# Plane stores issued by ScalarE, joint planes, and other places for fills, tile ends and the first projection's weights in an encoder layer

## The chip, the cores and the metric

The kernel runs on one core of a Trainium2 chip. A core has a matrix engine (TensorE, here PE, with PEld for its weight loads), VectorE (DVE), ScalarE (ACT), GpSimd (POOL) and SyncE (SP). SP computes nothing: it only issues DMA transfers, in the order of its queue, and waits before an issue until what the transfer reads is made and its place is free. ACT can issue transfers too, between its own operations. The metric is the device time of one execution in microseconds (us).

## The reference

Ten tiles of 128 tokens (1024 sample and 256 prompt tokens), model width 1024, hidden width 2816 (22 blocks of 128), pass one encoder layer:

```python
def swiglu(x, w_gu, w_down):
    g, u = jnp.split(x @ w_gu, 2, axis=-1)
    return (jax.nn.silu(g) * u) @ w_down

x = x + 0.5 * rmsnorm(swiglu(rmsnorm(x, ffn1_pre), ffn1_w_gu, ffn1_w_down), ffn1_post)
h = rmsnorm(x, mix_pre)
proj = h @ w_in
...
oa = window_gqa(qa, ka, va, sink_a)
...
mix = jnp.concatenate([rmsnorm(oa, out_norm_a), rmsnorm(ob, out_norm_b)], axis=-1) @ w_out
x = x + rmsnorm(mix, mix_post)
x = x + 0.5 * rmsnorm(swiglu(rmsnorm(x, ffn2_pre), ffn2_w_gu, ffn2_w_down), ffn2_post)
return rmsnorm(x, final_norm)
```

`window_gqa` (attention A) uses rotary queries and keys; `neighbourhood_attn` (attention B) adds a learned bias table.

## The kernel before

Products run in pairs of rounded float32 numbers: `split` makes `hi` with an ACT copy and `lo` as the difference on DVE (or POOL), and every product takes three matmuls (hi·hi, hi·lo, lo·hi).

**Gate/up.** Each block f of 128 hidden columns is computed with seven products instead of eight (a Strassen scheme over the halves of the model width and of gate and up), for two chunks of tokens: chunk 0 has 256, chunk 1 has 384. A block is 14 steps, n = 7·chunk + j. `prep(f+1)` splits the next block's weights into `ah`, `al` during these steps; they come by `load(f+2)` into one of two buffers for each half, at the end of block f. Four PSUM banks serve a chunk's seven products (`BANK`): product 2 uses product 0's bank again, so ACT must first have copied `u` out (L291). Then DVE adds, ACT applies Silu, and the results `w` and `v` of the block are stored (L319) as planes in DRAM (`hd`), `w` at j = 5, `v` at j = 6. For f ≥ 11 the planes of block f - 11 are fetched back (L327, tile `back`), and POOL makes four sums (`sums`, L336 to L339), stored as `s1` to `s4`.

**Weight sums.** The down product is a seven-product scheme too, and needs sums of weight blocks: `weight_sums` loads `bx` and two `bt`, makes four sums on POOL and returns the stores of T1 to T4 into `td`. In FFN1 sums i = f // 2 are made in every odd block f, and stored behind the next store of a plane. Tiles share tags: `t` (two buffers) serves `bt`, the table's tiles `cm` and `z`, and the raw down weights `rawd`; `x` (three buffers) serves `bx`, `back`, the residual `xr` and the first `h` tiles.

**Bias tables.** `bias_tables` makes the table for attention B in DRAM during FFN1; `fill` copies pieces of `zd` and a constant `neg` into `tt`, `fill_p` copies `zp` into `ttp`. Part of these fills is handed to attention A.

**Down.** 35 pairs (product q of 7, pair of tiles p of 5) of two pieces m (six and five k-blocks), 70 numbers n. `load_w` loads and splits a weight (`rawd` to `wd`), `load_h` loads a piece of a plane (`hl`) and splits it (`hh`). When q = 4 and q = 6 end for a pair, a tile is done: `tile_done` scales by the row factor (`row_factor`, POOL, L161 and L162) and adds the residual `xr`, then `finish1` stores the row (`x1d`), normalizes it for the projection and transposes it on PE, or `finish2` writes the output.

**Mix.** The input projection (`product`, matmuls `pj`) takes weights in pieces of 128 columns: raw weights `mraw` in the pool `mixr`, split `mh` and `ml` in `mixw`. Attention A runs as a pipeline of units with projection steps and fills between them; in `rope`, four small transfers `qs<-qf` swap halves, and DVE waits for them (L691).

**What sets the order.** The code is traced in program order for each engine; a list scheduler then moves an instruction ahead where its operands allow, as far as `issue_after` (an order given by hand) and the reuse of buffers let it. All transfers are in SP's queue and are issued in its order. Thus many constant fills of `tt` stand early in SP's queue, between FFN1's loads. The bank order, `queued` and the hook for the weight sums read:

```python
    BANK = (0, 1, 0, 2, 3, 2, 3)
...
        with self.tc.issue_after(self.last_store.ins):
            while fs:
                fs.pop(0)()
...
            with tc.issue_after(gu.last_load.ins):
                gu.later += d.weight_sums(sums)
```

## Time and profile before

| what | value |
|---|---|
| median of 3 runs | 2387.31 us (2383.97 to 2388.11) |
| profiled execution, its own time | 2389.29 us |
| its span in the profile | 2387.5 us |
| mean granted clock of TensorE | 0.978 |
| FFN1 gate/up, blocks 0 to 21 | 22 to 627 us |
| FFN1 down, first to last matmul | 643.2 to 919.2 us |
| mix (projection, attention A and B, output projection) | 919 to about 1527 us |
| FFN2 gate/up | 1527 to 2097 us |
| FFN2 down, first to last matmul | 2100.1 to 2371.4 us |

Rows of the profile read as follows: a group gives line, engine, operation, output and inputs, count, then busy time and the mean of one in ns, then the engine's idle time before them and what ended it. A row of waits gives the waiting engine and line, what it waited for, the sum, the number of times and the longest. A row of the timeline gives start and length in us; a bracket gives idle time before it and its end's cause. SPq is SP's queue.

### The profile page before, as it was taken

To read this page: it belongs to the slowest core of one execution; us is meant where nothing else is said; L and a number is where in the kernel's file an instruction comes from. 1 tells how busy PE (TensorE), PEld (TensorE's weight loads), DVE (VectorE), ACT (ScalarE), POOL (GpSimd) and SP (SyncE) were. 2 spreads that over 40 slices of the span, in tenths; PEclk is the share of its full clock that TensorE was granted. 3 is DMA by queue.
4 is the path that set the end of the run, shared out by engine and by line. 5 is a ranking of instruction groups with operands and counts; after the bars stand their busy time and mean duration, and the time that the engine had idled before them with its cause. 6 is when DMAs were issued, how large, how long until landed. Compare 5 with 4: busy or idle time off the path is not lost.

```text
span 2387.5 us, 37173 instructions
## 1 busy us (share of the span) xinstructions
PE 2255.3 (94%) x13328; PEld 2063.8 (86%) x13328; DVE 1447.7 (61%) x2565; ACT 966.7 (40%) x1993; POOL 691.5 (29%) x812
## 2 busy tenths in 40 slices
PE   5899999999799998999999999799999999999997
PEld 5899999999688886788888788699999999978875
DVE  6656556656345764498655756666656666544575
ACT  5322222222244443488666754332222222243453
POOL 5111104444200102487343334622122333300011
PEclk8999999999899998999999999899999999999999
DMA  4455657677765653322433545434544655575573
GB/s 142 108 143 140 149 145 210 181 216 215 226 198 172 218 192 124 84 47 60 116 108 83 151 137 181 163 121 136 168 153 150 178 149 161 143 256 171 173 250 116
DMA packets 421322, 371.98 MB, mean 156 GB/s; under 512 B 71633, under 2 KB 340817, under 8 KB 421137
## 3 DMA queue, kind: packets, MB, share of 16 engines
q1 hardware_dynamic: 421136, 369.61, 52.1%
q8 instruction: 105, 1.72, 0.3%
q14 instruction: 81, 0.66, 0.1%
HBM read 249.85 MB, written 121.90 MB: 156 GB/s over the span
## 4 chain that ended last, share of the span: by engine, by line
PE 71%; DVE 7%; DMA 5%; issue 3%; ACT 3%; POOL 3%; SPq 1%; DVEq 0%; ACTq 0%; POOLq 0%
PE gups L279 35%; PE dps L455 16%; PE pj L615 10%; PE yps L1087 2%; PE s_ps L644 2%; PE pt L654 2%; DMA raw<-in_ffn_w_gu_dram 1%; ACT junk L153 1%; POOL rs L162 1%; DVE al L71 1%; PE o_ps L771 1%; DMA rawd<-in_ffn_w_down_dram 1%; PE ssq L1072 1%; POOL rs L161 1%; DMA td0T<-bt 1%
## 5 line engine op out<-in xcount | busy, mean ns | idle before, releaser
L279 PE MATMUL gups<-xh,ah 128*128 128x256 f32 (+1 forms) x2464 | 767.8, 312 | 25.7 <-ACT u L291 13.1
L279 PE MATMUL gups<-xh,al 128*128 128x256 f32 (+1 forms) x2464 | 763.4, 310 | 1.7 <-DVE al L71 1.7
L279 PE MATMUL gups<-xl,ah 128*128 128x256 f32 (+1 forms) x2464 | 763.2, 310 | 0.0
L279 PEld LDWEIGHTS gups<-xh,ah 128*128 128x128 f32 x2464 | 468.6, 190 | 33.0 <-ACT u L291 15.1
L455 PE MATMUL dps<-wd,hh 128*128 128x512 f32 x1540 | 479.5, 393 | 17.8 <-ACT hh L68 17.8
L279 PEld LDWEIGHTS gups<-xh,al 128*128 128x128 f32 x2464 | 468.2, 190 | 2.2 <-DVE al L71 2.1
L279 PEld LDWEIGHTS gups<-xl,ah 128*128 128x128 f32 x2464 | 469.0, 190 | 0.0
L455 PEld LDWEIGHTS dps<-wd,hh 128*128 128x128 f32 x1540 | 289.7, 189 | 79.6 <-ACT hh L68 19.3
L455 PE MATMUL dps<-wd,hl 128*128 128x512 f32 x770 | 303.4, 394 | 5.1 <-DVE hl L71 5.0
L68 ACT ACTIVATE ah<-s 128x512 fp32r<-128x512 f32 x176 | 111.2, 632 | 230.7 <-PE gups L279 128.9
L68 ACT ACTIVATE hh<-hl 128x640 fp32r<-128x640 f32 (+1 forms) x140 | 110.8, 792 | 217.7 <-DMA hl<-hd1s 65.5
L71 DVE TENSOR_TENSOR al<-s,ah 128x512 fp32r<-128x512 f32 x176 | 142.0, 807 | 81.1 <-ACT ah L68 80.0
L71 DVE TENSOR_TENSOR hl<-hl,hh 128x640 fp32r<-128x640 f32 (+1 forms) x140 | 125.0, 894 | 97.5 <-ACT hh L68 96.3
L455 PEld LDWEIGHTS dps<-wd,hl 128*128 128x128 f32 x770 | 145.1, 188 | 41.5 <-DVE hl L71 9.6
L638 POOL TENSOR_TENSOR sb<-sb,rc 128x384 f32<-128x384 f32 (+1 forms) x160 | 126.5, 811 | 154.9 <-DVE rc L636 138.4
L615 PE MATMUL pj<-xh,mh 128*128 128x512 f32 (+1 forms) x432 | 162.2, 376 | 6.4 <-ACT mh L68 6.2
L615 PE MATMUL pj<-xh,ml 128*128 128x512 f32 (+1 forms) x432 | 156.2, 362 | 0.1
L615 PE MATMUL pj<-xl,mh 128*128 128x512 f32 (+1 forms) x432 | 156.0, 361 | 0.0
L306 ACT ACTIVATE u<-u 128x256 f32<-128x256 f32 x88 | 41.4, 471 | 276.4 <-DVE u L288 273.6
L68 ACT ACTIVATE ah<-raw 128x512 fp32r<-128x512 f32 x132 | 83.3, 631 | 151.0 <-PE gups L279 101.5
L71 DVE TENSOR_TENSOR wd<-rawd,wd 128x512 fp32r<-128x512 f32 x154 | 106.2, 692 | 56.3 <-ACT wd L68 55.9
L161 POOL TENSOR_SCALAR rs<-ssq 128x1 f32<-128x1 f32 x20 | 10.0, 500 | 433.5 <-ACT junk L472 433.4
(180 smaller groups left out, 3612.5 us busy)
## 6 DMA issues: line engine op xcount, KB each, us to landing
raw<-in_ffn_w_gu_dram SPq DMA_DIRECT2D x88, 512.0 KB, 4.4
rawd<-in_ffn_w_down_dram SPq DMA_DIRECT2D x66, 256.0 KB, 3.6
bx<-in_ffn_w_down_dram SPq DMA_DIRECT2D x22, 512.0 KB, 5.2
bt<-in_ffn_w_down_dram SPq DMA_DIRECT2D x44, 256.0 KB, 3.9
rawd<-td0T SPq DMA_DIRECT2D x44, 256.0 KB, 3.3
rawd<-td1T SPq DMA_DIRECT2D x44, 256.0 KB, 3.2
tab<-tt SPq DMA_DIRECT2D x24, 384.0 KB, 3.8
hl<-hd0s SPq DMA_DIRECT2D x20, 384.0 KB, 3.2
```

The lines of the kernel that those rows point to most:

```text
L68: nc.scalar.activation(hi, src, AF.Copy)
L71: (lo_eng or nc.vector).tensor_tensor(lo, src, hi.bitcast(F32), op=ALU.subtract)
L153: c.nc.scalar.activation(junk[:, :x.shape[1]], x, AF.Square, scale=1 / 32, accum_out=ss)
L161: nc.gpsimd.tensor_scalar(r, sums[0], sums[1] if len(sums) == 2 else 0.0, EPS, op0=ALU.add, op1=ALU.add)
L279: nc.tensor.matmul(ps, w[:, k, :], x[:, k, :], start=new and k == 0 and m == 0, stop=k == 3 and m == 2, skip_group_check=not new)
L306: nc.scalar.activation(X["u"], X["u"], AF.Silu)
L455: nc.tensor.matmul(ps, a[:, k, :], b, start=i == 0 and v == 0, stop=i == HF - 1 and v == 2)
L615: state["mm"] = nc.tensor.matmul(ps[:, :n], w[:, kk, :], xs[th][:, kk, :], start=first, stop=last)
L638: nc.gpsimd.tensor_tensor(s, s, rc[:, i:i + 1].to_broadcast(list(s.shape)), op=ALU.mult)
L644: nc.tensor.matmul(o, q, kk, start=z == 0, stop=z == 1)
L654: nc.tensor.transpose(pt[:, b, :], sbs[i][:, b * 128:(b + 1) * 128], c.ident)
L1087: nc.tensor.matmul(ps, a[:, j, i * 128:i * 128 + 128], b, start=j == 0 and m == 0, stop=j == 3 and m == 2)
```

## The change

1. Stores of planes, of weight sums, of `x1d` and of the outputs are issued by ACT, `w` behind the second Silu, `v` behind the next `u`, sums and weight sums behind `g` (`queued` now follows `last_act`). A fetch is put behind the last weight load.
2. Planes are joined: (w0, v0), (s2, s1), (s3, s4) and T2 with T1, one transfer each.
3. FFN1's weight sums are made in blocks 1, 2, 4, ..., 20; in both FFNs their stores are held until the next block. The first `h` is loaded in block 21.
4. The table's remaining fills are put behind the last `qs` transfer of a rope in attention A.
5. In the down phase the gains are loaded earlier; the gain multiply of one half comes at q = 3 and 5, and of the other when a tile is done; scale and residual are one operation; squares come in halves; the last scale of `finish2` is shared between DVE and ACT.
6. The last two tiles, 4 and 6, go by DMA into the `xl` buffer and are transposed behind the first two projections' products for thirds 0 and 2. The first projection's weights are loaded at n = 60 and split at n = 64; the pools of raw and split weights alternate with one buffer each.

ACT's queue around two chunk ends in the second half of FFN1's gate/up (`ah` and `u` are the names above, `td0T` a weight sum's store, the numbers are buffers). Before:

```order
L306 ACTIVATE u<-u 128x384
L291 ACTIVATE u<-gups 128x256
L295 ACTIVATE g<-gups 128x256
L68 ACTIVATE ah<-raw 128x512
L306 ACTIVATE u<-u 128x256
L291 ACTIVATE u<-gups 128x384
L68 ACTIVATE ah<-s_5930 128x512
L68 ACTIVATE ah<-raw 128x512
L68 ACTIVATE ah<-s_5929 128x512
L295 ACTIVATE g<-gups 128x384
```

And ACT's queue now, from `v`'s store of chunk 0 in such a block to `w`'s store of chunk 1:

```order
L319 DMA hd0v_107<-v 128x2x128
L69 ACTIVATE ah<-raw 128x512
L69 ACTIVATE ah<-s_5837 128x512
L296 ACTIVATE g<-gups 128x384
L319 DMA hd0s_111<-back 128x4x128
L319 DMA hd0s_115<-sums 128x4x128
L69 ACTIVATE ah<-s_5882 128x512
L69 ACTIVATE ah<-raw 128x512
L69 ACTIVATE ah<-s_5838 128x512
L69 ACTIVATE ah<-raw 128x512
L306 ACTIVATE u<-u 128x384
L319 DMA hd0w_104<-w 128x3x128
```

The stores stand between ACT's own operations: `hd0s`, which waits for POOL's sums, ahead of four splits, and `hd0w` between Silu and the next `u`.

SP's queue at the end of FFN1's gate/up (`td0T` stores of weight sums, `rawd` and `hl` the first loads of the down phase). Before:

```order
L401 DMA td0T_193<-bt 128x512
L401 DMA td0T_171<-bx 128x512
L401 DMA td0T_182<-bx 128x512
L401 DMA td0T_204<-bt 128x512
L411 DMA rawd<-in_ffn_w_down_dram 128x512
L319 DMA hd0v_112<-v 128x3x128
L319 DMA hd0s_124<-sums 128x3x128
L411 DMA rawd<-in_ffn_w_down_dram 128x512
L319 DMA hd0s_116<-back 128x3x128
L319 DMA hd0s_120<-back 128x3x128
L411 DMA rawd<-in_ffn_w_down_dram 128x512
```

And now, from block 20's loads for the weight sums on:

```order
L400 DMA bt<-in_ffn_w_down_dram 128x512
L401 DMA bt<-in_ffn_w_down_dram 128x512
L396 DMA bx<-in_ffn_w_down_dram 128x1024
L326 DMA back<-hd0w_99 128x4x128
L326 DMA back<-hd0w_100 128x6x128
L416 DMA rawd<-in_ffn_w_down_dram 128x512
L446 DMA hl<-hd0w_97 128x768
L416 DMA rawd<-in_ffn_w_down_dram 128x512 x7
L446 DMA hl<-hd0w_99 128x640
```

No store stands between the loads any more; the first loads of the down phase follow the last fetch.

PE's queue at the end of FFN1's down phase (`dps` down products, `tr` transposes of normalized rows, `pj` projection). Before:

```order
L455 MATMUL dps<-wd,hh 128x512 x2
L455 MATMUL dps<-wd,hl 128x512
L1364 MATMUL tr<-ident,u_7143 128x128 x4
L1364 MATMUL tr<-ident,c_6914 128x128 x4
L1364 MATMUL tr<-ident,u_7199 128x128 x4
L615 MATMUL pj<-xh_8542,mh 128x512
L615 MATMUL pj<-xl_8543,mh 128x512
```

And now:

```order
L462 MATMUL dps<-wd,hh 128x512 x2
L462 MATMUL dps<-wd,hl 128x512
L1412 MATMUL tr<-ident,u_7020 128x128 x4
L636 MATMUL pj<-xh_8437,mh 128x512
L636 MATMUL pj<-xl_8438,mh 128x512
```

One group of four transposes stands between the last down product and the first projection, where there were three.

The diff, cut to what is spoken of:

```diff
-PLANES = ("w0", "v0", "w1", "v1", "s1", "s2", "s3", "s4")
+PLANES = (("w0", "v0"), ("w1",), ("v1",), ("s2", "s1"), ("s3", "s4"))
...
+    def store(self, names, f, ch, h):
-        self.last_store = self.c.nc.sync.dma_start(self.plane(name, f, ch), h.rearrange("p (r x) -> p r x", x=128))
+        self.c.nc.scalar.dma_start(self.plane(names, f, ch), h.rearrange("p (r x) -> p r x", x=128))
...
-        for b, name in zip(self.back[f, ch], ("w0", "v0")):
-            self.c.nc.sync.dma_start(b.rearrange("p (r x) -> p r x", x=128), self.plane(name, f, ch))
+        with self.tc.issue_after(self.last_load.ins):
+            self.c.nc.sync.dma_start(x.rearrange("p (r x) -> p r x", x=128), self.plane(("w0", "v0"), f, ch))
...
-        with self.tc.issue_after(self.last_store.ins):
+        with self.tc.issue_after(self.last_act.ins):
             while fs:
                 fs.pop(0)()
...
             self.product(f, ch, j)
-            if j == 5:
+            if j == 0:
+                self.queued(self.last_v)
+            if j == 4:
                 self.queued(self.later)
             if j == 6:
+                w, v = self.X["w"], self.X["v"]
+                self.queued([lambda: self.store(("w" + k,), f, ch, w)])
+                self.last_v.append(lambda: self.store(("v" + k,), f, ch, v))
...
-        return [lambda a=a: nc.sync.dma_start(self.td[a[0]][i], a[1]) for a in (("T3", b22), ("T1", b12), ("T2", b11), ("T4", b21))]
+        return [lambda a=a: nc.scalar.dma_start(self.td[a[0]][i], a[1]) for a in (("T3", b22), ("T21", x), ("T4", b21))]
...
+def split_win(c, pool, raw):
+    hi, lo = [pool.tile([128, 8, 128], F32R, name=n) for n in ("mh", "ml")]
...
+            if n == 0:
+                st["w"] = pre
+            else:
+                pool = mw if n % 2 else mr
+                st["w"] = split_win(c, pool, load_win(nc, pool, w_in, cols))
...
+    def pinned(f):
+        with tc.issue_after(state["pin"].ins):
+            f()
...
             with tc.issue_after(gu.last_load.ins):
-                gu.later += d.weight_sums(sums)
+                gu.held = d.weight_sums(sums)
+
+        def release():
+            gu.later += gu.held
+            gu.held = []
...
+        also(3, release)
         if sums is not None:
-            hooks[8] = behind
+            also(8, behind)
...
+            also(12, lambda: d.load_h(0))
...
+        gu.queued(gu.last_v)
         gu.queued(gu.later)
-        d.load_h(0)
         d.load_w(0, HF - 1)
+        d.ap = R.open("acc", 1)
         d.hp = R.open("h", 1)
-        d.ap = R.open("acc", 1)
...
+            if m and q in (3, 5):
+                y, h = d.acc[p]["c21" if q == 3 else "u"], slice(0, 512) if q == 3 else slice(512, 1024)
+                nc.vector.tensor_tensor(y, y, gpost[:, h], op=ALU.mult)
...
-        for y, h in halves:
-            nc.vector.scalar_tensor_tensor(y, y, r, gpost[:, h], op0=ALU.mult, op1=ALU.mult)
+        nc.vector.tensor_tensor(y, A[b if second else a], gpost[:, h], op=ALU.mult)
+        r = row_factor(c, [A[a, "ss"], A[b, "ss"]])
         yield 1
-        for y, h in halves:
-            nc.vector.tensor_tensor(x[:, h], x[:, h], y, op=ALU.add)
-        yield from finish(t, x, gnext, halves)
+        for z, h in zip((A[a], y) if second else (y, A[b]), halves):
+            nc.vector.scalar_tensor_tensor(x[:, h], z, r, x[:, h], op0=ALU.mult, op1=ALU.add)
+            ss.append(square(c, x[:, h], junk_bank()))
...
-        gu.run(f, block_hooks(gu, f, {6: behind} if 1 < f < HF else {}, f // 2 if f % 2 else None))
+        gu.run(f, block_hooks(gu, f, {6: behind} if 1 < f < HF else {}, f // 2 if f == 1 or f % 2 == 0 else None))
...
+    def first_split():
+        state["pre"] = split_win(c, state["mr"], state["raw"])
...
-        elif t == PAIRS[-1][0]:
+            if t in (PAIRS[-2][0], PAIRS[-1][0]):
...
+        for _, h in halves:
+            nc.vector.tensor_tensor(x[:, h], x[:, h], gain[:, h], op=ALU.mult)
+        r = row_factor(c, ss)
...
+        nc.vector.tensor_scalar(x[:, a], x[:, a], r, None, op0=ALU.mult)
+        nc.scalar.activation(x[:, b], x[:, b], AF.Copy, scale=r)
```

More of the change, by code (lines that the diff above doesn't have):

```diff
@@ L178, in __init__ @@
         self.xb = [[None] * 7 for _ in CHUNKS]
-        self.A, self.raw, self.back, self.later = {}, {}, {}, []
+        self.A, self.raw, self.back, self.later, self.held, self.last_v = {}, {}, {}, [], [], []
         self.work = None
@@ L581, in load_win, with parts @@
     return raw
+def split_win(c, pool, raw):
+    hi, lo = [pool.tile([128, 8, 128], F32R, name=n) for n in ("mh", "ml")]
+    def parts():
+        for k in range(0, 8, 2):
+            split(c, hi[:, k:k + 2], lo[:, k:k + 2], raw[:, k:k + 2], c.nc.gpsimd)
+            yield
+    return hi, lo, parts()
 def mix_attention(c, tc, xt, w_in, sink, cosT, sinT, maskA, tt, ttp, oAd, oBd, mw, L, R,
-                  close_left, open_out, late, mr, raws, fills):
+                  close_left, open_out, late, mr, pre, fills):
     nc = c.nc
@@ L591, in mix_attention @@
     ready = set()
+    count = {"n": 0}
     def product(cols, evac):
@@ L598, in fetch @@
         def fetch():
-            st["raw"] = raws.pop(cols[0][0]) if cols[0][0] in raws else load_win(nc, mr, w_in, cols)
-            st["w"] = [mw.tile([128, 8, 128], F32R, name=n) for n in ("mh", "ml")]
+            n = count["n"]
+            count["n"] += 1
+            if n == 0:
[3 more added lines that the diff above has]
+                st["w"] = split_win(c, pool, load_win(nc, pool, w_in, cols))
         def part(i):
-            hi, lo = st["w"]
-            s = slice(2 * i, 2 * i + 2)
-            split(c, hi[:, s], lo[:, s], st["raw"][:, s], nc.gpsimd)
+            next(st["w"][2], None)
         def mm(th, k0):
             n = TH[th][1]
-            hi, lo = st["w"]
+            hi, lo, _ = st["w"]
             if k0 == 0:
@@ L1229, in down_phase @@
             q, p, m = d.seq[n]
-            if n == 30:
-                gpost = load_gain(c, G, post, "ga", scale=0.5)
-                gnext = load_gain(c, G, nxt, "gb")
-            if n == 60:
-                last()
+            if n == 20:
+                with tc.issue_after(d.last_h.ins):
+                    gpost = load_gain(c, G, post, "ga", scale=0.5)
+                    gnext = load_gain(c, G, nxt, "gb")
+            if n in last:
+                last[n]()
             if m == 0 and q in (4, 6):
@@ L1376, in finish1 @@
         yield 1
-        xn = [y for y, _ in halves]
-        if "xt" not in state:
-            state["xn"][t] = xn
-        elif t == PAIRS[-1][0]:
-            th, off = third(t)
-            x = state["xt"][1][th][:, :, off:off + 128].bitcast(F32)
-            for k, y in enumerate(xn):
-                nc.sync.dma_start(x[:, 4 * k:4 * k + 4], y.rearrange("p (k x) -> p k x", x=128))
-            state["xn"][t] = [x[:, 4 * k:4 * k + 4] for k in range(2)]
-            state["late"] = transposes(t)
-        else:
-            state["xn"][t] = xn
-            yield from transposes(t)
-    down_phase(gu, lambda t: rows(xs, xp, t), i["ffn1_post"], i["mix_pre"], finish1, open_xt)
+        xn = state["xn"][t] = [y for y, _ in halves]
+        if "xt" in state:
+            if t in (PAIRS[-2][0], PAIRS[-1][0]):
+                th, off = third(t)
+                x = state["xt"][1][th][:, :, off:off + 128].bitcast(F32)
+                for k, y in enumerate(xn):
+                    nc.sync.dma_start(x[:, 4 * k:4 * k + 4], y.rearrange("p (k x) -> p k x", x=128))
+                state["xn"][t] = [x[:, 4 * k:4 * k + 4] for k in range(2)]
+                state["late"].append(transposes(t))
+            else:
+                yield from transposes(t)
+    down_phase(gu, lambda t: rows(xs, xp, t), i["ffn1_post"], i["mix_pre"], finish1, {60: open_xt, 64: first_split})
     R.close(4)
-    mw = L.open("mixw", 2)
+    mw = L.open("mixw", 1)
     mo = MixOut(c, L, R, i["w_out"][0], (i["out_norm_a"], i["out_norm_b"]), oAd, oBd, x1d, x2d, xnd, i["mix_post"], i["ffn2_pre"])
@@ L1398, in encoder @@
     mix_attention(c, tc, state["xt"], i["w_in"][0], i["sink_a"], i["cosT"], i["sinT"], i["maskA"], tt, ttp, oAd, oBd,
-                  mw, L, R, lambda: L.close(4), mo.open, lambda: list(state["late"]), state["mr"], state["raws"], later)
+                  mw, L, R, lambda: L.close(4), mo.open, lambda: [list(x) for x in state["late"]], state["mr"], state["pre"], later)
     c.ps.use(y=(2, 3, 4, 5), tr=(6, 7, 0, 1))
```

96 lines of the change are left out of this document (51 added, 45 removed).

## The prediction

> **What bounds the kernel now.** I read the page's first and fourth parts, then tables of stretches, then the waits, then single stretches of the timeline.
>
> ```profile
> PE 2255.3 (94%) x13328; PEld 2063.8 (86%) x13328; DVE 1447.7 (61%) x2565; ACT 966.7 (40%) x1993; POOL 691.5 (29%) x812
> PE 71%; DVE 7%; DMA 5%; issue 3%; ACT 3%; POOL 3%; SPq 1%; DVEq 0%; ACTq 0%; POOLq 0%
> ```
>
> PE holds 71% of the chain, and the change leaves its matmuls as they are. What can be won is PE's idle time, 2387.5 - 2255.3 = 132 us, and the lower clock behind long gaps. A table of stretches (start and end, length, then busy time of PE, PEld, DVE, ACT, POOL, granted clock, DMA share, GB/s) finds the places:
>
> ```profile
> 82.70:626.90 544.20, 522.31 (x3529) 516.60 (x3527) 316.23 (x520) 139.18 (x271) 154.55 (x137) 0.99 0.64 173
> 627.00:643.30 16.30, 0.23 (x2) 0.09 (x1) 3.63 (x6) 3.40 (x6) 4.70 (x5) 0.65 0.93 280
> 643.30:650.00 6.70, 6.70 (x18) 5.03 (x19) 4.58 (x6) 3.67 (x6) 0.00 (x0) 0.59 0.94 303
> 920.00:940.00 20.00, 9.34 (x26) 6.62 (x27) 10.36 (x15) 7.41 (x18) 8.63 (x14) 0.57 0.34 115
> 1000.00:1140.00 140.00, 136.13 (x856) 119.00 (x857) 125.01 (x363) 116.21 (x327) 102.77 (x178) 0.98 0.26 57
> 1578.80:2096.90 518.10, 516.71 (x3517) 515.73 (x3515) 314.86 (x523) 146.45 (x276) 141.21 (x129) 1.00 0.52 158
> 2371.40:2387.50 16.10, 0.00 (x0) 0.00 (x0) 6.53 (x10) 3.02 (x6) 2.44 (x6) 0.64 0.18 65
> ```
>
> The first and sixth rows are blocks 1 to 21 of gate/up in FFN1 and in FFN2, the same matmuls: 544.2 against 518.1, so FFN1 loses **26.1 us**. The second and third are the passage into FFN1's down phase: 16.1 idle, then 6.7 us at clock 0.59, of which 41% or 2.8 are lost. The fourth is the passage out of it: 10.7 idle, some 3 more to the clock. The fifth is attention A, where DVE is busy 125 of 140 us. The last is the tail, 16.1 without a matmul.
>
> Why FFN1 loses is in the groups of that stretch (count, busy time, mean ns, idle time before and what ended it):
>
> ```profile
> L279 PE MATMUL gups<-xh,ah 128*128 128x256 f32 (+1 forms) x1176 | 365.4, 311 | 20.2 <-ACT u L291 12.7 <-DVE v L288 7.3
> L68 ACT ACTIVATE ah<-raw 128x512 fp32r<-128x512 f32 x60 | 37.7, 628 | 73.9 <-DMA raw<-in_ffn_w_gu_dram 45.5 <-PE gups L279 28.4
> ```
>
> PE waits for `u`, which ACT copies out of the bank that the third product needs; ACT waits for the next block's weights, whose splits stand ahead of that copy. One such stall in the timeline, SP's queue, then ACT, and two rows of SP's waits:
>
> ```profile
> 157.69 0.38 SPq L228 DMA_DIRECT2D raw<-in_ffn_w_gu_dram  x1
> 158.11 5.36 SPq L550 DMA_DIRECT2D tt<-in_neg_dram  x1
> 163.56 0.56 SPq L319 DMA_DIRECT2D hd0w<-w  x1
> ...
> 169.65 0.66 SPq L228 DMA_DIRECT2D raw<-in_ffn_w_gu_dram  x1
> 167.34 0.63 ACT L68 ACTIVATE ah<-raw 128x512 fp32r<-128x512 f32 x1 [5.92 <-DMA raw<-in_ffn_w_gu_dram]
> 168.29 0.36 ACT L291 ACTIVATE u<-gups 128x256 f32<-128x256 f32 x1
> SPq L319 <- DVE w L302: 261.7, 63, 11.7
> SPq L228 <- DVE s L257: 154.9, 28, 20.1
> ```
>
> The first weight load was issued at 157.69 and its split began 9.65 later, with a fill and stores beside it; the second load came behind them, 12 us after the first. In all SP stood 261.7 us at stores whose `w` was not made yet, with loads queued behind.
>
> **The change, term by term,** against the profiled run (span 2387.5, its own time 2389.3, which is 2.0 above the median shown and 1.2 above the highest).
>
> *Gate/up of FFN1.* Stores leave SP, so a weight load waits for its own buffer alone. A block of the second half had 12 stores and 4 fetches of planes and now has 8 and 2, of the same bytes, and 11 table fills, 17 constant ones and 16 small ones leave for attention A. Of the 26.1, block 1 keeps about 4: its loads go out behind block 0, at 82.7, which the change leaves. New in even blocks 12 to 20: ACT stands at the `hd0s` stores until POOL's four sums are made, with four splits and `u` behind, and POOL now has four weight sums ahead of them. Estimated from the block's start: `bx` waits about 8 us for its buffer and lands in 5 to 6 (row below), eight POOL operations take 8 x 1.13 (154.55 / 137) = 9, four splits 4 x 0.63 = 2.5: 25 to 26. PE needs `u` at 24.5 + 2 x 1.4 = 27.3 (a block, then two products of 256 of 640 columns, 24.5 x 0.4 / 7 each), less 0.4 for the copy. The margin is 1 with a scatter of 2, so I charge 0.8 five times, 4. Gain 26 - 4 - 4 = **-18** (-7 to -26). What the store alone delays at a chunk's end:
>
> ```profile
> bx<-in_ffn_w_down_dram SPq DMA_DIRECT2D x22, 512.0 KB, 5.2
> L319 SPq DMA_DIRECT2D hd0w<-w x44: 359/384/2207, 59.6 to 626.3; - x44
> 602.76 0.52 ACT L306 ACTIVATE u<-u 128x384 f32<-128x384 f32 x1 [2.51 <-DVE u L288]
> 603.58 0.38 ACT L291 ACTIVATE u<-gups 128x256 f32<-128x256 f32 x1 [0.30 <-PE gups L279]
> ```
>
> An issue of 0.38 us goes between these two, where ACT is idle for 0.30; PE asks for `u` 1.4 us after it could start, 1.0 after the copy's end, so some 0.9 of slack stays and the median costs nothing. The longest, 2.2, costs 2.2 - 0.3 - 1.0 = 0.9. No row shows a joint store's issue: by two single ones it is 0.8, still inside, and it stands at a place with more room (behind `g`). FFN2 gets these stores as well, and its row has 1.4 us idle in 518: **+1** (0 to 5, a few long issues).
>
> *Into FFN1's down phase.* Before, the loads of the first `rawd` wait for the buffers of td's last stores:
>
> ```profile
> 630.54 0.39 SPq L401 DMA_DIRECT2D td0T<-bt  x1
> 635.26 0.63 ACT L68 ACTIVATE wd<-rawd 128x512 fp32r<-128x512 f32 x1 [6.97 <-DMA rawd<-in_ffn_w_down_dram]
> 642.32 0.84 ACT L68 ACTIVATE hh<-hl 128x768 fp32r<-128x768 f32 x1 [0.98 <-DMA rawd<-in_ffn_w_down_dram]
> ```
>
> Now the last weight sums are block 20's, stored early in block 21, and ten loads and the first `hl` come during block 21, as in FFN2. So PE starts at once. Late next is `hh` of the second piece: on ACT it stands behind the last `hd0s` stores, which wait for four POOL sums behind the last `v`. From the last `gups`: 1.5 for `v`, 4 x 1.1 for the sums, 0.9 for two issues, 0.8 for `hh`, so 8; PE's first piece has 18 matmuls at 0.227 (30.2 / 133, a row below), 4.1. Idle 4, clock and the next weights 4: 19 becomes 8, **-11** (-4 to -17). FFN2's passage, in the same order:
>
> ```profile
> 2096.90:2110.00 13.10, 11.20 (x50) 9.01 (x51) 8.50 (x12) 5.00 (x8) 3.38 (x3) 1.00 0.77 228
> 2100.10:2133.50 33.40, 31.16 (x135) 24.53 (x134) 15.87 (x21) 14.50 (x23) 3.38 (x3) 1.00 0.89 281
> 721.20:751.40 30.20, 30.20 (x133) 24.79 (x132) 14.52 (x20) 10.59 (x17) 0.00 (x0) 1.00 0.53 167
> ```
>
> There four pairs end 36.6 us after the last `gups`, where four undisturbed ones (last row) take 30.2: 6.4 lost, which is also a check on the 8. It too loses stores in front of its loads, and gets the same `hh` behind stores: **-2.5** (+2 to -5).
>
> The Trainium skill, "TensorE: Matmul & The Clock Gate", section "What's actually happening", has the clock fall to half after an idle window of about 3.4 us. The trace agrees as far as it goes: 0.59 behind the gap of 16.1, 1.00 in FFN2's passage with short ones. By that rule an idle time of 4 in one piece may cost clock, and in shorter pieces the sum would be some 2 us lower.
>
> *Down pairs.* Where DVE fills up, pairs stretch; four that took 30.2 above take here:
>
> ```profile
> 819.10:852.00 32.90, 31.59 (x138) 25.09 (x137) 29.93 (x46) 18.64 (x34) 8.48 (x14) 1.00 0.84 281
> ```
>
> DVE is busy 29.9 of 32.9. A tile's work on it stays about as long (four operations, gain multiplies and sums in another pairing), but one gain multiply moves ahead to q = 3 and 5. **-3** for both FFNs (+3, if the order only shifts the crowd, to -6).
>
> *Out of the down phase.* Two waits of PE:
>
> ```profile
> PE tr L1364 <- DVE c L1375: 4.5, 1, 4.5
> PE pj L615 <- ACT mh L68: 6.2, 1, 6.2
> ```
>
> Both go: the transposes of the last two tiles stand behind projection products, and the first projection's weights are split within the down phase. Late next are the second projection's weights: their buffer lies where the last `h` tiles are, so the load goes out behind the last matmul. PE has 24 matmuls of the first projection, 24 x 0.227 = 5.4, and four transposes; the load of 512 KB takes 4 to 5 (as `bx`), its first split under 1. So 0 to 3 of 13.7 stay: **-12** (-4 to -14).
>
> *Attention A* gets the 44 fills, on the queue that carries its ropes' transfers:
>
> ```profile
> L688 SPq DMA_DIRECT2D qs<-qf x60: 507/582/1349, 973.1 to 1100.8; - x60
> tt<-in_neg_dram SPq DMA_DIRECT2D x7, 192.0 KB, 9.3
> ```
>
> 60 transfers are 15 ropes in 128 us, one every 8.5. A fill goes out behind one rope's transfers and took up to 9.3 to land in FFN1 (share 0.64); at 0.26 it should be gone before the next rope. DVE has 15 of 140 us to hide what is left. **+3** (0 to +12, 1 us at twelve ropes).
>
> *Tail.*
>
> ```profile
> 2374.20 1.41 DVE L1469 SCALAR_TENSOR_TENSOR xr<-xr,rs,gb 128x512 f32<-128x512 f32 x2 [2.31 <-POOL rs L162]
> 2375.53 0.68 DVE L466 TENSOR_TENSOR c<-c,dps 128x512 f32<-128x512 f32 x1
> ```
>
> The last sum `c` starts 4.1 us after the last matmul (2371.4), behind the tile before it, whose last DVE step waits for `rs`; now less of that tile is left. Gain and addition merge (about 1.4 less), the last multiply is shared with ACT (0.7 less): **-6** (-3 to -7.5).
>
> Sum: -18 + 1 - 11 - 2.5 - 3 - 12 + 3 - 6 = -48.5; 2389.3 - 48.5 = 2340.8, and about 1 less on the median's scale: **2340**.
>
> **Rivals.** (a) *The loads stay late*, because the 16 engines and not SP's order set their landing. For it: 9.65 us above, and share 0.64 in FFN1; against it: the fills leave FFN1, and FFN2 at 0.52 has no stall. Gate/up then gains 5 and the passage 6: 2340 + 13 + 5 = 2358. The Trainium skill, "DMA: Bandwidth & Descriptors", section "Issuing engines are not separate DMA queues", is on this side: a second issuer saves only the time to initiate a transfer. The rows of SP's waits show another cost, order in one queue. (b) *Fills hit the ropes* at twelve of 15: +12 in place of +3, 2349. (c) *The new place does not do what it is for*: ACT's waits at `hd0s` hold `hh` until the passage is as long as before (+11), and hold `u` 3 us in each of five blocks (+11): 2362. (d) *Slower*: issues on ACT take longer than the 0.3 + 1.0 us of room at each of 88 chunk ends. All 49 us are gone at 0.55 more than that, an issue of 1.85 every time; at 2.2 it costs 88 x 0.9 = 79, and the time is 2419. For it speaks the maximum of 2.2 and the 5.36 of a fill; against it the median of 0.38.
>
> **Numbers.** Forecast (2322 to 2349) 0.63; (a) 0.15; (b) 0.09; (c) 0.08; (d) 0.04; 0.01 for anything else. A measurement of this kernel tells about 0.2% (5 us) from no change. Of (a), (c) and the rest 0.04 may run on to within 0.2%, which leaves faster 0.92, same 0.04, slower 0.04. The range 2322 to 2366 takes in (a), (b) and (c); the low end has 18 us more, with gate/up, the passage and the pairs near their best.
>
> **What would show it.** Right: FFN1's 21 blocks in under 530 us and ACT's wait for `raw` below 20; the first `dps` within 2 us of the last `gups`, then one gap on `hh` below 6; `pj` straight behind `tr`; a tail near 10. Wrong: `u` released by a store or by POOL; `qs` waits of DVE in attention A above 10 us; FFN2's 21 blocks above 525; `raw` landing in 8 us without fills beside it.

## The result and the profile after

The changed kernel takes **2403.39 us** (median of 4 runs, 2403.16 to 2406.25), the kernel before 2386.39 on the same chip (4 runs, 2383.97 to 2388.11). The ratio is 1.0075, 95% interval 1.0057 to 1.0092: slower by 0.75%, where 2340 and faster had been predicted. The profiled execution has a span of 2401.4 us, 13.9 above that of before.

First the table of stretches after (start and end, length, busy time of PE, PEld, DVE, ACT, POOL, clock, DMA share, GB/s): blocks 1 to 21 of gate/up in FFN1, the first down pair, attention A, blocks 1 to 21 in FFN2, its first down pair, the tail.

```profile
77.20:609.50 532.30, 518.91 (x3530) 515.05 (x3529) 322.33 (x522) 143.25 (x274) 162.55 (x138) 1.00 0.62 168
609.80:622.80 13.00, 10.72 (x35) 7.93 (x35) 6.75 (x10) 4.98 (x9) 3.58 (x3) 0.79 0.81 259
959.10:1163.60 204.50, 168.20 (x893) 139.24 (x894) 130.41 (x371) 122.73 (x335) 98.36 (x179) 0.86 0.34 77
1594.10:2112.20 518.10, 518.10 (x3529) 517.77 (x3529) 320.22 (x528) 147.60 (x277) 148.02 (x129) 1.00 0.53 158
2112.40:2128.20 15.80, 10.18 (x34) 7.73 (x33) 5.57 (x9) 4.48 (x7) 3.02 (x3) 0.78 0.59 193
2388.40:2401.40 13.00, 0.08 (x1) 0.00 (x0) 5.90 (x10) 3.80 (x10) 3.56 (x6) 0.70 0.22 81
```

Two stretches of before in the same table, attention A from its first `s_ps` to its last `o_ps`, and FFN2's blocks 1 to 21:

```profile
1000.10:1146.50 146.40, 142.63 (x894) 124.60 (x895) 128.48 (x371) 119.38 (x335) 103.66 (x179) 0.98 0.25 56
1578.80:2099.90 521.10, 518.68 (x3528) 517.71 (x3527) 317.86 (x528) 148.65 (x279) 141.21 (x129) 1.00 0.52 158
```

Attention A runs the same matmuls 58.1 us longer. PE idles 204.5 - 168.2 = 36.3 instead of 3.8 us, and its busy time is 25.6 longer, at a clock of 0.86 instead of 0.98. All else together got 44 us shorter. By stage, cut at PE's first and last matmuls (us; the parts of the mix that are left out differ by 0.3 together):

| stage | before | after | difference | predicted |
|---|---|---|---|---|
| start to end of FFN1 gate/up | 626.8 | 609.5 | -17.3 | -18 |
| passage and first down pair, FFN1 | 16.4 + 10.3 | 0.3 + 13.0 | -13.4 | -11 |
| other 34 pairs, FFN1 | 265.3 | 268.8 | +3.5 | -1.5 |
| out of the down phase | 13.9 | 0.6 | -13.3 | -12 |
| **attention A** | 146.4 | 204.5 | **+58.1** | +3 |
| FFN2 gate/up, all blocks | 572.5 | 567.5 | -5.0 | +1 |
| passage and first down pair, FFN2 | 0.2 + 9.0 | 0.2 + 15.9 | +6.9 | -2.5 |
| other 34 pairs, FFN2 | 262.0 | 259.8 | -2.2 | -1.5 |
| tail | 16.5 | 13.3 | -3.2 | -6 |

The groups of FFN1's blocks after, as shown of before:

```profile
L280 PE MATMUL gups<-xh,ah 128*128 128x256 f32 (+1 forms) x1176 | 363.9, 309 | 13.4 <-DVE v L289 11.9 <-ACT u L292 1.0 <-ACT ah L69 0.5
L69 ACT ACTIVATE ah<-raw 128x512 fp32r<-128x512 f32 x60 | 37.8, 631 | 61.8 <-PE gups L280 58.4 <-DMA raw<-in_ffn_w_gu_dram 2.3 <-issue 1.1
```

ACT's wait for `raw` fell from 45.5 to 2.3, and PE's for `u` from 12.7 to 1.0: the stall of the prediction is gone. In attention A, PE's two largest waits, then the transfers in that stretch (KB each, median us to landing):

```profile
PE o_ps L792 <- DVE st L687: 14.2, 8, 3.6
PE s_ps L665 <- DVE stk L72: 12.9, 7, 3.3
...
tt<-zd SPq DMA_DIRECT2D x11, 384.0 KB, 7.9
...
tt<-in_neg_dram SPq DMA_DIRECT2D x6, 192.0 KB, 17.5
```

PE waits for DVE, with DVE itself busy 130 of 204 us. DVE's own two largest waits in that stretch are for engines, and none that the profile shows there is for a rope's `qs`:

```profile
DVE pl L72 <- ACT ph L69: 32.7, 26, 6.8
DVE qf L714 <- POOL qf L711: 15.6, 7, 4.4
```

DVE's queue at one rope, after and then before:

```profile
1018.65 1.30 DVE L712 TENSOR_TENSOR qs<-qs,sin 128x512 f32<-128x512 f32 x1
1019.88 0.41 DVE L687 TENSOR_TENSOR st<-o_ps,of 64x256 f32<-64x256 f32 x1
1022.67 0.69 DVE L714 TENSOR_TENSOR qf<-qf,qs 128x512 f32<-128x512 f32 x1 [2.39 <-POOL qf L711]
1024.06 1.41 DVE L72 TENSOR_TENSOR stk<-qf,stk 64x512 fp32r<-64x512 f32 x2 [0.69 <-ACT stk L69]
```

```profile
1030.11 0.79 DVE L691 TENSOR_TENSOR qs<-qs,sin 128x512 f32<-128x512 f32 x1
1031.00 0.56 DVE L71 TENSOR_TENSOR pl<-pt,ph 128x384 fp32r<-128x384 f32 x1
...
1032.68 0.67 DVE L693 TENSOR_TENSOR qf<-qf,qs 128x512 f32<-128x512 f32 x1
1033.27 0.74 DVE L71 TENSOR_TENSOR pl<-pt,ph 128x256 fp32r<-128x256 f32 x2
...
1035.57 2.19 DVE L71 TENSOR_TENSOR stk<-qf,stk 64x512 fp32r<-64x512 f32 x2 [0.68 <-ACT stk L68]
```

Before, a rope's links stood apart, with the softmax of other units between them. After, only one `st` stands between them, and DVE waits for POOL and ACT inside the chain. So two things changed in attention A: slow fills are in it, and every engine's order is another. The change orders only the fills by hand; the rest of the loop is left to the scheduler. The experiments had to tell the two apart.

### The profile page after: what moved, and what is told of

The parts are those of the page before. It is cut to its first block, busy times and chain, and to the rows that moved or that the text cites. A ratio compares the mean times of both kernels' runs of the same rounds, so it can differ in the third digit from the quotient of the medians.

```text
span 2401.4 us, 36895 instructions
## 1 busy us (share of the span) xinstructions
PE 2273.8 (95%) x13328; PEld 2072.3 (86%) x13328; DVE 1458.6 (61%) x2575; ACT 982.4 (41%) x2043; POOL 709.0 (30%) x812
## 3 DMA queue, kind: packets, MB, share of 16 engines
q10 hardware_dynamic: 130688, 91.25, 12.4%
## 5 line engine op out<-in xcount | busy, mean ns | idle before, releaser
L280 PE MATMUL gups<-xh,ah 128*128 128x256 f32 (+1 forms) x2464 | 764.9, 311 | 18.6 <-DVE v L289 13.5
L280 PEld LDWEIGHTS gups<-xh,ah 128*128 128x128 f32 x2464 | 466.7, 189 | 24.5 <-DVE v L289 15.8
L69 ACT ACTIVATE hh<-hl 128x768 fp32r<-128x768 f32 (+1 forms) x140 | 110.6, 791 | 209.6 <-DMA hl<-hd0s 55.3
L72 DVE TENSOR_TENSOR hl<-hl,hh 128x768 fp32r<-128x768 f32 (+1 forms) x140 | 124.6, 891 | 106.3 <-ACT hh L69 106.3
L462 PEld LDWEIGHTS dps<-wd,hl 128*128 128x128 f32 x770 | 145.8, 189 | 44.2 <-DVE hl L72 12.6
```

What stands on the lines that cost most here:

```text
L69: nc.scalar.activation(hi, src, AF.Copy)
L72: (lo_eng or nc.vector).tensor_tensor(lo, src, hi.bitcast(F32), op=ALU.subtract)
L280: nc.tensor.matmul(ps, w[:, k, :], x[:, k, :], start=new and k == 0 and m == 0, stop=k == 3 and m == 2, skip_group_check=not new)
L462: nc.tensor.matmul(ps, a[:, k, :], b, start=i == 0 and v == 0, stop=i == HF - 1 and v == 2)
```

## The experiments

The stages of all runs (us; cut as above; time is the median or that of one run; the last column is the kernel before on the same chip, and the experiments come from four chips). Pinned fills are those that the change puts behind a rope's last `qs`. The new orders are those that the engines have in attention A with pinned fills, the old ones those without:

| run | FFN1 gate/up | down 1 | att. A | down 2 | time | before |
|---|---|---|---|---|---|---|
| changed kernel | 609.5 | 281.8 | 204.5 | 275.7 | 2403.4 | 2386.4 |
| e1 fills not pinned | 635.4 | 284.2 | 146.1 | 274.5 | 2372.8 | 2384.2 |
| e6 e1, PE's new order | 633.0 | 285.1 | 180.1 | 274.6 | 2402.8 | 2384.2 |
| e2 pinned, PE's old order | 607.5 | 283.8 | 205.6 | 274.4 | 2403.5 | 2384.2 |
| e3 changed, `h` pool first | 607.7 | 283.4 | 204.1 | 265.4 | 2392.3 | 2384.2 |
| e7 constants in FFN1 | 631.8 | 287.0 | 202.5 | 267.6 | 2421.1 | 2385.7 |
| e8 fills in down 1 | 610.2 | 349.6 | 146.5 | 266.2 | 2403.3 | 2385.7 |
| e9 e8, stores on SP | 620.4 | 342.3 | 145.4 | 265.6 | 2405.4 | 2385.7 |
| e10 fills issued by ACT | 609.2 | 284.9 | 207.6 | 267.7 | 2400.1 | 2393.5 |
| e12 only constants pinned | 618.1 | 283.6 | 184.0 | 267.8 | 2387.6 | 2393.5 |
| e13 e1 with `h` first | 645.3 | 282.2 | 145.3 | 265.6 | 2370.0 | 2393.5 |
| e14 third `st` buffer | 610.7 | 284.6 | 199.1 | 266.6 | 2391.1 | 2384.1 |
| e15 constants read from `zd` | 608.6 | 283.3 | 192.1 | 267.0 | 2381.3 | 2384.1 |
| e17 pinned, four old orders | 609.3 | 282.8 | 205.2 | 266.7 | 2398.2 | 2385.2 |
| e18 no fills, four new orders | 637.4 | 285.8 | 202.9 | 267.0 | 2423.8 | 2385.2 |
| **e19 e17, constant rows** | 611.0 | 284.0 | 158.2 | 266.5 | **2350.2** | 2385.2 |
| e20 e13, constant rows | 623.7 | 283.3 | 146.3 | 265.6 | 2350.7 | 2385.2 |
| e21 e8, constant rows | 612.4 | 304.4 | 145.8 | 267.0 | 2360.6 | 2388.4 |
| e16 e13, old tile end | 647.6 | 279.7 | 146.4 | 269.8 | 2379.6 | 2388.4 |

### Are the pins the cause? e1, e6, e2

```diff
 e1
-                    todo.insert(4 * n + 3, (0.0, lambda f=fills.pop(0): pinned(f)))
+                    todo.insert(4 * n + 3, (0.0, fills.pop(0)))
 e6: e1, and e2: the changed kernel, both with an order for PE
+    with given_order(tc, mybir.EngineType.PE, ORDER):
         for j in range(4):
```

> The changed kernel, its table fills not put behind the ropes: the scheduler places them in FFN1 again, and PE's order in attention A is the one of before. Theory O (the fills behind the ropes made the scheduler give PE another order, projection products in runs of up to 27, and PE idles later) and theory T (the fills' transfers and their issues hold up the small transfers of attention A) both say: attention A, from the first s_ps to the last o_ps, goes from 204.5 back to 146 to 150 us. FFN1's gate/up, which ends at 609.5, then shows what the fills cost there: 0 to 15 us more. Time 2345 to 2360. If neither holds (the weight pools of one buffer each, or the stores on ACT, slow attention A), it stays near 200 and the time near 2400.

> The kernel of e1_no_pin (no fills in attention A), with PE's order in attention A given by hand as the changed kernel has it, instruction for instruction. Theory O: attention A takes 190 to 205 us with no fill near it. Theory T: 146 to 152.

> The changed kernel, fills behind the ropes, with PE's order in attention A given by hand as the kernel before has it. Theory O: attention A takes 146 to 155 us although all fills run beside it. Theory T: 190 to 205. If both have a part, the two runs split the 58 us.

e1 puts the fills (43 in the trace: 11 copies from `zd`, 16 constant ones, 16 copies from `zp`) back where the scheduler had them, in FFN1. Attention A is whole again, FFN1's gate/up ends 26 us later, above the 0 to 15 expected, and the kernel beats the one before: 2372.8 us, not the 2345 to 2360 expected, ratio 0.9951 (0.9936 to 0.9965). So the pins cost the 58, and FFN1's gain hangs on the fills' leaving: with them back its gate/up is 8.6 longer than in the kernel before. e6 and e2 did not separate order and fills: PE's new order alone costs 34, and with PE's old order the fills still cost 59. They hold one engine's order; the other three stayed with the scheduler.

### FFN2's first pair: e3

```profile
2096.29 0.33 SPq L446 DMA_DIRECT2D hl<-hd1w  x1
2101.55 9.18 SPq L416 DMA_DIRECT2D rawd<-in_ffn_w_down_dram  x5
2118.21 0.82 SPq L446 DMA_DIRECT2D hl<-hd1w  x2
```

```profile
SPq L446 <- POOL sums L337: 2.9, 1, 2.9
SPq L446 <- DMA hd1w<-w: 2.6, 1, 2.6
```

These are SP's queue and its waits in the changed kernel around FFN2's passage: the second `hl` goes out 6 us behind the last `gups`, because its place is that of gate/up's work tiles, whose sums POOL has yet to make and whose stores have yet to land. The change had swapped the opening of the pools `h` and `acc`, which moved `h` onto them. The edit swaps it back in FFN2:

```diff
+        if last:
+            d.ap = R.open("acc", 1)
         d.hp = R.open("h", 1)
+        if not last:
+            d.ap = R.open("acc", 1)
```

> The changed kernel, with the pool of h opened before that of the sums again in FFN2's down phase (in FFN1 as changed). Theory P (the swapped pools put h over the gate/up tiles, so the first loads of h wait for the last stores and sums): the first pair of FFN2's down phase, 15.9 us, goes to 8 to 10 and the gap of 5.6 goes; the time is 6 to 8 us below the changed kernel's. Theory A (hh stands on ACT behind the last stores): the first pair stays at 14 to 16.

FFN2's first pair fell from 15.86 to 7.49 us, and down 2 from 275.7 to 265.4; the time of this one run fell by 11, more than the 6 to 8 expected. The place of `h` was the cause. All runs below have this edit. In FFN1 the pools stay as in the change, and the first pair stays at 12.4 to 14.6 us, but for e9 (9.2, below).

### What a fill costs, and where: e7, e12, e8, e10, e14

```diff
 e7: the constant parts not pinned, zd and zp pinned; e12 the reverse, with PE's old order
+    for f in fills:
+        f(z=False)
+    fills = [lambda f=f: f(neg_=False) for f in fills]
 e8: nothing in attention A; in FFN1's down phase
+    {60: open_xt, 64: first_split, **{8 + 3 * n: f for n, f in enumerate(later)}}
 e10: e2 with the fills issued by ACT
-        nc.sync.dma_start(tf[:, :, a, rh, e0 * 32:e0 * 32 + 256], ...)
+        e.dma_start(tf[:, :, a, rh, e0 * 32:e0 * 32 + 256], ...)
 e14: e2 with
+        st = k.tile([64, 256], F32, name="st", bufs=3)
```

> The changed kernel with h's pool first in FFN2's down phase (as e3_h_first), and of the fills behind the ropes only the copies from zd and zp left there; the constant ones (tt<-neg) are placed by the scheduler, early in FFN1. Theory N (the constant fills, which take 13 to 17 us to land, clog the transfers wherever they are): attention A falls from 204.5 to 150 to 170 us, and FFN1's gate/up, which ended at 609.5, ends 10 to 25 us later. Theory Z (any fill on SP's queue holds up attention A's stores and rope transfers): attention A stays at 180 to 205 and gate/up ends near 612.

> The reverse of e7_neg_early, with PE's order of before: the constant fills (tt<-neg) behind the ropes, the copies from zd and zp placed by the scheduler, in FFN1. From e7 (gate/up to 631.8 with the constant ones early) the constant fills cost FFN1 about 22 us and the copies about 4; so gate/up should end at 610 to 616. Attention A: e7 had 202.5 with the copies alone; if the constant fills are harmless there it takes 146 to 155, if any fill costs there, 165 to 190.

> The changed kernel with h's pool first in FFN2's down phase and the 15 groups of fills issued by SP in FFN1's down phase, one at every third of 70 steps from step 8, each behind the load of the newest h. Theory P (fills cost where short transfers are waited for within a few us; the down phase has its next pieces loaded ahead): gate/up ends at 607 to 612, the down phase takes 282 to 295 us, attention A 146 to 150, FFN2's first pair 7.5; time 2335 to 2350. Theory T (44 fills cost 26 to 58 us wherever they run): the down phase takes 310 to 340 us; time 2360 to 2390.

> The kernel of e2_pinned_old_order (fills behind the ropes in attention A, PE's order of before) with h's pool first in FFN2, and the fills of attention A issued by ACT, behind the rope's first copy, in place of SP. Theory S (on SP's queue the fills stand ahead of the stores oAd<-st and the rope's qs, whose landings they hold up; e2 took 205.6 us there): with another queue attention A falls to 150 to 170 us, and oAd lands in at most 6 us. Theory E (the 16 DMA engines are filled, whichever queue issues; or ACT, busy 119 of 146 us, is held up by the issues): it stays at 185 to 215.

> The kernel with pinned fills and PE's old order in attention A (attention A 205.6 us there), h pool opened first in FFN2, and a third buffer for the tile st that oAd's stores read. Theory 'buffer': the fills stall attention A through late oAd stores that keep st's two buffers (DVE st <- DMA oAd 9.2, PE o_ps <- DVE st 35.5); with three buffers most of that goes, attention A 165 to 185, total about 2375. Theory 'everywhere': what is late is every short transfer of the ropes and outputs, and the wait only moves to qs and the clock; attention A stays 195 to 206, total about 2393. FFN2's first pair near 7.5 us in both.

e7: the constant parts alone cost FFN1 24 us (631.8 against 607.7), and attention A, with the copies alone, still takes 202.5. That is not the copies' doing. They and what runs beside them land fast in e7, and DVE's largest wait is that of the changed kernel:

```profile
tt<-zd SPq DMA_DIRECT2D x11, 384.0 KB, 4.1
oAd<-st SPq DMA_DIRECT2D x39, 64.0 KB, 2.1
DVE pl L72 <- ACT ph L69: 32.7, 26, 7.7
```

The engines' orders in e7 are the new ones, but for a few swaps, so what e7 measures is those. e12 has the constants alone, with 184.0; e10 and e14 have all fills. These three have PE's old order and the scheduler's for the other engines, so they too price fill and order together.

e8: 349.6 against about 283 without fills, and attention A whole (146.5). So the down phase was no cheap place. The Trainium skill, "DMA: Bandwidth & Descriptors", section "Issuing engines are not separate DMA queues", has transfers of every issuer run on the same 16 engines, so that a second issuer saves only the time to start one. e10 agrees: with the fills issued by ACT attention A takes 207.6 against 205.6 us, and the constant ones of 192 KB still land in 14.6. So it is not SP's queue that makes them slow. (e9, below, shows a gain of another kind from a second issuer: loads that no longer stand behind stores.) e14: a third buffer for `st` brings 6.5 us of the 59, so the stall is not that one buffer.

### Order or transfers: e15, e17, e18, e19

e15 reads the constants from rows of `zd`, so each row from an address of its own, and its table lacks the constant. e17 and e18 hold PE, DVE, ACT and POOL, in the projection and attention A, to the order of the other case. e19 is e17 with 384 constant rows in DRAM:

```diff
 e15
-                nc.sync.dma_start(tf[:, :, a, rh, lo * 32:hi * 32], src)
+                nc.sync.dma_start(tf[:, :, a, rh, lo * 32:hi * 32], zf[:, :, 384:384 + n])
 e17 (pinned fills), e18 (fills not pinned)
+    with given_order(tc, ORDER):
         with in_order(tc, mybir.EngineType.DVE):
 e19
-                src = bass.AP(tensor=neg.tensor, offset=neg.offset, ap=[[0, 16], [0, 24], [1, n]])
+                src = neg.rearrange("(q x) n -> q x n", x=24)[:, :, :n]
```

> As the run with pinned fills and PE's old order (attention A 205.6 us), h pool first in FFN2, but the constant fills of tt (early and pinned ones) read rows of zd, each from an address of its own, in place of the one constant row read 384 times; rows, sizes and places written are the same, the table's constant entries are wrong. Theory 'one source': many reads of the same few hundred bytes are what is slow; landing of these fills falls from 10 to 17 us to below 5, oAd's longest from 16 to below 8, attention A to 160 to 180 (the zd copies still cost some), gate/up of FFN1 5 to 10 earlier. Theory 'small rows': 384 rows of 128 to 512 bytes written to scattered places are slow whatever is read; landing stays 9 to 17 and attention A 195 to 210.

> Pinned fills in attention A as in the change, h pool first in FFN2, and the orders of PE, DVE, ACT and POOL in the projection and attention A held to those of the kernel without pins. Theory 'order': the scheduler, which counts the pinned fills as time, put the engines' work in a bad order, and the transfers themselves cost little; attention A 146 to 160, total 2335 to 2350, the fastest so far. Theory 'transfers': the fills' own traffic delays oAd and qs whatever the order; attention A 190 to 206, total 2385 to 2395. Between them (165 to 185) both count.

> The reverse: no fill in attention A (they are in FFN1, whose gate/up then takes about 640), h pool first in FFN2, and PE, DVE, ACT and POOL in the projection and attention A held to the orders that the pinned fills gave. Theory 'order': attention A 190 to 205, total about 2420. Theory 'transfers': 146 to 155, total about 2372. TensorE's new order alone had given 180.

> As e17, with the constant as 384 rows in DRAM, so that each row of a constant fill of tt reads an address of its own; the table is right. Theory 'one source': oAd's and qs's longest landings fall below 6 us; attention A falls to 146 to 150 if e17 is above it, and is within 3 of e17 if e17 is near 150. FFN1's gate/up, which keeps 17 constant fills, 0 to 6 us earlier than in e17 (609).

Transfers in attention A in e17, then in e19 (KB each, median us to landing):

```profile
tt<-zd SPq DMA_DIRECT2D x11, 384.0 KB, 7.7
oAd<-st SPq DMA_DIRECT2D x38, 64.0 KB, 2.4
qs<-qf SPq DMA_DIRECT2D x24, 64.0 KB, 4.9
tt<-in_neg_dram SPq DMA_DIRECT2D x6, 192.0 KB, 16.2
```

```profile
tt<-zd SPq DMA_DIRECT2D x11, 384.0 KB, 3.9
oAd<-st SPq DMA_DIRECT2D x38, 64.0 KB, 2.1
qs<-qf SPq DMA_DIRECT2D x24, 64.0 KB, 2.0
tt<-in_neg_dram SPq DMA_DIRECT2D x6, 192.0 KB, 4.3
```

The same bytes to the same places land in 4.3 instead of 16.2 us when each row has a source of its own, and the `zd` copies beside them in half the time. Fills from one row cost attention A 59.9 us under the old orders (e17 against e13). DVE's waits in attention A, first e17, then e18, then e19's row for the same transfers:

```profile
DVE qs L786 <- DMA qs<-qf: 24.8, 4, 11.4
DVE st L761 <- DMA oAd<-st: 22.3, 6, 5.1
```

```profile
DVE pl L72 <- ACT ph L69: 32.5, 25, 7.7
DVE qf L806 <- POOL qf L803: 14.6, 7, 4.4
```

```profile
DVE qs L786 <- DMA qs<-qf: 2.3, 3, 1.0
```

Attention A by fills and orders:

| | old orders | new orders |
|---|---|---|
| no fills | 145.3 (e13) | 202.9 (e18) |
| fills from one row | 205.2 (e17) | 204.1 (e3) |
| only copies from `zd` and `zp` | not run | 202.5 (e7) |
| fills from 384 rows | 158.2 (e19) | not run |

Each cause is enough alone, by its own waits: in e17 DVE waits for transfers, in e18 for engines, with no fill near. They don't add, and so a run that takes away one alone finds little. In the changed kernel the waits are those of e18: its orders hide the slow fills. With both gone the fills cost 13 us, above the 146 to 150 us expected for attention A. Most of that is one wait of ACT in e19, which PE then waits for, for weights of the projection that SP issues behind the last fills:

```profile
ACT mh L69 <- DMA mraw<-in_w_in_dram: 12.1, 1, 12.1
```

In e15 the fills land in about 4 us too, but attention A takes 192.1 in place of the 160 to 180 expected, with PE's old order and the other engines' left to the scheduler. The stretch in e19, against the changed kernel's row above:

```profile
963.10:1121.20 158.10, 141.78 (x893) 123.16 (x894) 128.31 (x371) 119.22 (x335) 103.54 (x179) 0.97 0.42 99
```

The DMA share is higher than in the changed kernel, 0.42 against 0.34. The share did not show this cost; the landings did.

e19 takes 2350.21 us (2349.03 to 2355.70), ratio 0.9860 (0.9845 to 0.9874), and is, with e20 (2350.73 in one run on the same chip), the fastest version measured.

### The same source in FFN1 and in the down phase: e20, e21

```diff
 e13, e8
-                src = bass.AP(tensor=neg.tensor, offset=neg.offset, ap=[[0, 16], [0, 24], [1, n]])
 e20, e21
+                src = neg.rearrange("(q x) n -> q x n", x=24)[:, :, :n]
```

> e1_no_pin and e3_h_first together: fills placed by the scheduler, h's pool first in FFN2's down phase. Each alone gave 2372.8 and 2392.3 (the changed kernel 2403.4), so if their gains of 30.6 and 11 add, 2362; if they share something, 2364 to 2372.

> The fills in FFN1 (unpinned, gate/up 635 to 645 us there, 609 without them), h pool first in FFN2, and the constant as 384 rows. Theory 'one source': the constant fills are what costs FFN1 its 26 to 35 us; gate/up ends at 610 to 620, total 2345 to 2355. Theory 'order of one queue, or bytes': gate/up stays 630 to 645, total about 2370.

> The fills in FFN1's down phase (349.6 us there with the one constant row, 282 to 287 without fills), h pool first in FFN2, the constant as 384 rows. Theory 'one source': down phase 284 to 300, attention A 146, gate/up 610; total 2336 to 2353, perhaps the fastest. Theory 'transfers in a busy place': h, w and fills share the engines and the down phase stays above 320; total above 2370.

ACT's wait in FFN1's blocks in e13, then in e20; last, PE's in the down phase in e8 and e21:

```profile
L69 ACT ACTIVATE ah<-raw 128x512 fp32r<-128x512 f32 x61 | 38.4, 630 | 75.4 <-PE gups L280 49.2 <-DMA raw<-in_ffn_w_gu_dram 18.0 <-DMA bx<-in_ffn_w_down_dram 3.0
```

```profile
L69 ACT ACTIVATE ah<-raw 128x512 fp32r<-128x512 f32 x61 | 38.4, 630 | 53.3 <-PE gups L280 48.5 <-issue 3.9 <-DVE al L72 0.6
```

```profile
PE dps L462 <- ACT hh L69: 53.5, 11, 11.3
```

```profile
PE dps L462 <- ACT hh L69: 12.3, 6, 3.2
```

FFN1's gate/up with unpinned fills varies between runs: e1, e6, e13, e16 and e18 have one order on every engine and in SP's queue there, and take 633.0 to 647.6. e20, in that same order and with only the source changed, takes 623.7, so the rows bring 9 to 24 us (14 against e18, on the same chip), and ACT's wait for `raw` falls from 18.0 to below the 0.6 of the last row shown. Some 14 remain, more than expected (610 to 620). In the down phase the cost falls from 66 to 21 (304.4 against 283), above the 300 expected. e13 was expected at 2362; it takes 2370.0, on a chip where the kernel before takes 2393.5, ratio 0.9905 (0.9889 to 0.9922). e21 has 0.9872 (0.9849 to 0.9895).

### ACT's stores alone, and the tile end: e9, e16

```diff
 e9: stores of planes and weight sums
-        self.c.nc.scalar.dma_start(self.plane(names, f, ch), ...)
+        self.last_store = self.c.nc.sync.dma_start(self.plane(names, f, ch), ...)
 e16: tile_done, finish1 and finish2 as before the change
-            if m and q in (3, 5):
-                nc.vector.tensor_tensor(y, y, gpost[:, h], op=ALU.mult)
```

> The kernel of e8_fills_down_sp with all stores of planes and weight sums issued by SP again, as before the change; planes joint, weight sums in even blocks and held. Theory F (FFN1's gate/up gained because the fills left it): gate/up ends at 605 to 615. Theory Q (it gained because the loads no longer stand behind stores in SP's queue): it ends at 618 to 630. FFN2's gate/up tells the same: 572.5 us before, 567.5 with the change.

> The kernel without pins and with the h pool first in FFN2 (down phases 282.2 and 265.6 us, tail 13.5), but with the tile end of before: both gain multiplies, the sums and the squares when a tile is done, outputs' last scale on DVE and stored by SP. Theory 'new tile end helps the tail alone': down phases within 1.5 of those, tail 15.5 to 16.5. Theory 'new tile end stretches the pairs' (an early gain multiply and two squares in ACT's and DVE's queues): down phases 3 to 5 shorter, tail 15.5 to 16.5. Theory of the prediction (pairs gain 1.5 for each FFN): down phases 1 to 3 longer.

With stores on SP, FFN1's gate/up is 10.2 us longer (620.4 against 610.2), with ACT waiting 23.7 us for `raw`; FFN2's is 568.6 against 568.0. But FFN1's down phase is 7.3 shorter (342.3 against 349.6, with the fills in both), 3.9 of it in the first pair, 9.2 in place of 13.1: `hh` no longer stands behind stores in ACT's queue, and PE's wait for it there falls from 2.6 to 0.5. So ACT's issue is worth 10 in FFN1's gate/up, gives some 4 of it back at the start of the down phase, and is worth nothing in FFN2.

The old tile end makes FFN2's down phase 2 to 4 us longer (269.8; the 14 runs with the new one and `h` first take 265.4 to 267.8) and the tail 3.4 (16.9 against 13.5). FFN1's down phase is 2.5 shorter than in e13, 1.0 of it in the first pair; other runs with the new tile end and no fills there take 281.8 to 287.0, so this is hardly more than their spread. None of the three theories holds in both phases.

## Why the prediction was wrong

**The step that failed** is the term "*Attention A* gets the 44 fills", +3 (0 to +12). Measured: 58.1. It asked what the fills do to ropes whose order stays. The order of attention A had changed on all four engines, and that alone costs 57.6 (e18 against e13); the changed kernel shows the waits of e18 and none for `qs`. The part ahead of the prediction says that a scheduler sets the order, but compares orders only in FFN1 and at the down phase's end; the prediction took that of attention A as given. Why the scheduler chose this one, I only argue: it seems to charge the fills to the queue that the ropes need, and so puts ropes late.

The price of the fills was wrong as well, and would have cost as much under the old orders (59.9, e17). The term took 9.3 us for the most that a fill needs to land in FFN1; the row's figure is a median, and the longest there took 20.7. It let this shrink at a DMA share of 0.26; in attention A it was 17.5. e19, e20 and e21 show that the slow landing belongs to the one source row, in each of three places. And it counted the ropes' `qs` alone, not the `oAd` stores, for which DVE waited 22.3 us in e17. Its count was off by one: the trace has 16 constant fills and not 17, so 43.

Rival (b), fills hit the ropes at +12, named one of the two mechanisms, at a fifth of its size; the changed kernel does not show it, since its orders hide it. Rival (d), slower by ACT's issues, gave the right sign by a wrong mechanism: nothing in the trace or e9 bears it out.

**FFN1 gate/up** (-18, measured -17.3): right in size, in part by luck. The term gave most of the gain to the stores' leaving SP's queue. Stores on ACT are worth 10 once the fills are gone (e9), but with the fills still in FFN1 the changed gate/up takes 633.0 to 647.6 (e6 to e16), 6 to 21 more than the 626.8 of before's one trace, and why was not tried. The fills' leaving makes 24 to 38. That block 1's start at 82.7 is one "which the change leaves" was wrong: it is 77.2, and 77.1 to 78.8 in every run whose constant fills leave FFN1, 81.7 to 82.6 where they stay; that is 5.5 of the 17.3. Blocks 1 to 21 took 532.3, above the 530 named as a sign of being right. The sum for `u` behind the `hd0s` stores is 24.5 to 25.5, not 25 to 26; PE waited 1.0 us for `u` in all, not the 4 charged. Rival (a), landings set by the 16 engines, was half right: the fills slowed what ran beside them, but SP's order counts too (e9).

**FFN2's comparison row** ended 3 us early, and so does the stage in the table of before: the last `gups` is at 2099.9, not 2096.9. So FFN2's blocks took 521.1, FFN1 lost 23 rather than 26.1, and the passage 3.4 rather than 6.4. The stores on ACT were to cost +1; the blocks went to 518.1 without idle time.

**Into FFN1's down phase** (-11, measured -13.4) and **out of it** (-12, -13.3): right, with the mechanism as told. The first pair still loses 5.5, to `hh` and the clock of 0.79, below the 8 charged; in e9, without stores ahead of `hh`, it loses 1.6.

**FFN2's passage** (-2.5, measured +6.9): the term counted the stores and overlooked the swapped pools, which stand in the diff. e3 takes back 8.4.

**Down pairs** (-3 for both, measured +3.5 and -2.2): right for FFN2 (e16: 2 to 4 by the tile end), wrong sign for FFN1, where e16 gives at most 1.5 of the +3.5 to the tile end. The rest wasn't tried apart.

**Tail** (-6, measured -3.2): right mechanism, half the size.

Without attention A's 58 and the pools' 8.4 the changed kernel would stand at 2403.4 - 66.5, about 2337, near the 2340 predicted. No run measures this, since the fills cost something wherever they were put; e19, with 13 for them, measures 2350.
